# Conditioning sums, load distance and the start of a recurrence in a two-block network

## Chip, cores and metric

One core of one Trainium2 chip runs the whole kernel as one program. The metric is device time in microseconds (us): the median of the runs of a kernel. Trace times below are us from the start of the span of one profiled execution.

## What is computed

An input of 256 rows by 1024 columns passes through two blocks in 32-bit floats. The first block has a sparse attention and convolution mixer and a gated feed-forward layer. The second has two layers of three sublayers: feed-forward, mixer, feed-forward. The mixer of its first layer is a differential attention, that of its second a gated linear recurrence. Shortened:

```
for layer in range(2):
    mod = (silu(c) @ ada_w[layer] + ada_b[layer]).reshape(1, 3, 3, 1024)   # shift, scale, gate of each sublayer
    x = x + 0.5*gate0 * swiglu(rms(x)*(1+scale0) + shift0)      # feed-forward
    h = rms(x)*(1+scale1) + shift1
    x = x + gate1 * (diff_attention(h) if layer == 0 else hgrn2(h))
    x = x + 0.5*gate2 * swiglu(rms(x)*(1+scale2) + shift2)      # feed-forward
```

The recurrence `hgrn2` has 8 heads of 128. Per head it needs a query product and a forget product of h. The forget gates decay a running state along the 256 rows, and the values are summed with these decays. A gate product and an output product follow.

## The kernel before

**Products.** TensorE multiplies with each operand split in a high and a low part: `whi` is ScalarE's cast of the weights (L200), `wlo` is VectorE's difference (L213), and each product is three matmuls (high by high, high by low, low by high). Weights come in 1 MB pieces through `Stream`, in one fixed order: five feed-forward layers of 33 pieces each, the attention's 16 pieces (`w_qk`, `w_v`, `w_o`), the recurrence's 20. `load_to` issues a load on SP's queue into the pool `raw`, which has five buffers. `next` (L216) hands out piece i, issues loads up to piece i + `loads` (2 unless said) and splits ahead.

**Conditioning sums.** The 24 vectors `mod` (shift, scale, gate) are weights times `silu(c)`. They are computed piece by piece beside the rest: one part of a vector is a 1 MB load (`adaraw`, L522, in the same five buffers and on the same queue) and two VectorE instructions of 128x1024 that add into `adacc` (L549 for the first of a vector, L551 for the others). Four parts make a vector. Then `reduce` sums over the partitions with TensorE (L571 for a gate, L574 for a shift or scale) and VectorE adds the bias. `ADA_PLAN` (L501) is a list of (step, parts): at each weight piece `ada_step` (L503) compares the parts loaded with a straight line through that list, loads at most one more, and sums at most one that was loaded in an earlier step. The step is the number of the weight piece plus 8. The attention's pieces are 74 to 89, so its steps are 82 to 97; those of the third and fourth feed-forward sublayer are 98 to 130 and 131 to 163.

**Which vector is reduced where.** Each sublayer gets lists of vectors: `early` for the feed-forward loop, reduced when their parts are summed, `scale` for a mixer's output product, reduced between its pieces (`out_product`), and `fill` for a sublayer's end. Parts 52 to 55 belong to vector 15, 56 to 59 to vector 16, 60 to 63 to vector 17, 68 to 71 to vector 19, 80 to 83 to vector 22. Vectors 15 and 16 are the shift and scale for the recurrence layer's first sublayer, needed at the end of the third feed-forward sublayer; 19 is needed at the end of the fourth.

**Attention.** Four times a product for two heads (`rows_half`, `ps_qk`), the sums of squares, a power on GpSimd (`qss`, L631), the normalised rows (`qk`, L1660), transposes (`ps_qkT`), scores, softmax (`s`, `a`), transposes. Then the value products and the output product. Here the planner orders the instructions of each engine by its own estimate of when they are due.

**Recurrence.** Its order is written by hand (`order(True)`) up to the end of its main loop; what stands behind the loop (gate and value products) the planner may issue between. Work goes by pairs of heads, g = 0 to 3. `heads(g)` makes the forget product (`ps_f`, four pieces of 12 matmuls) and the query product (`ps_q`, four pieces) and computes the forget gates on ScalarE and VectorE in steps between the query's pieces. Pair 0 runs through `heads(0)` alone. Then a loop over g takes the diagonal product (`ps_d`, L1855) and eight levels: exponentials on ScalarE (`hX`, L1865), products and prefix sums on VectorE (L1867 to L1873), one piece of later pairs' work (`next(fill)`, L1875), and a product of the level (`ps_l`, L1882, at the last level L1885) that VectorE copies under a mask. `work` deals out pairs 1 to 3, 24 pieces in all, over the 32 levels.

Of the kernel before, what the change touches and what calls it, by code (L numbers as in the profile page):

```python
# [168 lines left out]
class Stream:  # L169
# [46 lines left out]
    def next(self, ahead=3, loads=2, ada=True):  # L216

        i = self.at
        self.at += 1
        self.split_to(2 * i + 1)  # L220
        self.load_to(i + loads)
        if ada:
            self.net.ada_step(i + 8)
        self.split_to(2 * i + 1 + ahead)
        self.load_to(i + loads)
        return [self.parts.pop(2 * i), self.parts.pop(2 * i + 1)]
# [188 lines left out]
class Net:  # L415
# [82 lines left out]
        mm(out, wl, xh, start=False, stop=last)  # L498


    ADA_PLAN = ((0, 0), (8, 0), (14, 12), (36, 24), (56, 36), (76, 48), (93, 60), (126, 72), (159, 84), (184, 84), (204, 88))  # L501

    def ada_step(self, i):  # L503
        for (a, na), (b, nb) in zip(self.ADA_PLAN, self.ADA_PLAN[1:]):
            if a <= i <= b:
                goal = na + (nb - na) * (i - a) / (b - a)
                break
        else:
            goal = 88
        before = self.ada_loaded  # L510
        if self.ada_loaded < min(goal, 88):
            self.ada_load()
        self.ada_to(min(before, self.ada_done + 1))
# [197 lines left out]
    def rows_half(self, name, done):  # L711

        acc = [self.psum("acc", f"{name}{t}") for t in range(2)]
        xh, xl = self.h
        for j in range(2):
            parts = self.W.next()
            for k in range(4):
                f = 4 * j + k
                for t in range(2):
                    self.rows_mm([acc[t]], parts[k // 2], t, (xh[:, f], xl[:, f]), f == 0, f == KT - 1, (k % 2) * 512)  # L720
        for t in range(2):
            done(t, acc[t])
# [1036 lines left out]
    def hgrn(self, end, scale, fill):  # L1759
        nc, T, tc, W = self.nc, self.T, self.tc, self.W  # L1760
        with ExitStack() as es:
# [7 lines left out]
            ac = m1.tile([P, 4, 2, P], F32, name="hac")  # L1769
            def product(name, done):  # L1770

                parts = W.next(ahead=1)
                ps = self.psum("acc", name)
                for n in range(2):
                    for piece in self.feat_pieces(ps, parts, n * S, n * P):
                        if n and piece == 0:
                            W.split_to(2 * W.at + 1)
                        if n and piece == 1:
                            done(ps)
                        yield  # L1780
# [44 lines left out]
            def work():  # L1825
                for g in range(1, 4):
                    yield from heads(g)
# [13 lines left out]
            if True:  # L1841
                for _ in heads(0):
                    pass
                nc.gpsimd.tensor_copy(levels, wide)
                fill = work()
                late = []
                for g in range(4):
                    (pre, suf, kk), q = gates.pop(g), qs.pop(g)
                    A = at[:, g].rearrange("p t e s -> p (t e) s")

                    pd = self.psum("t", "ps_d")
                    for t in range(2):
                        for e in range(2):
                            o = (2 * t + e) * P
                            nc.tensor.matmul(pd[:, o:o + P], kk[:, e, t * P:(t + 1) * P], q[:, e, t * P:(t + 1) * P], start=True, stop=True)  # L1855

                    def diagonal(A=A, pd=pd):
                        nc.vector.tensor_tensor(out=A, in0=pd.rearrange("p (a b) -> p a b", a=4),
                                                in1=self.ident[:, None, :].to_broadcast([P, 4, P]), op=ALU.mult)
                    late.append(diagonal)  # L1860
                    for a, m in enumerate(LEVELS + (P,)):
                        nb = 2 * S // (2 * m)
                        blk = lambda x: x.rearrange("p a b -> p (a b)").rearrange("p (n c) -> p n c", c=2 * m)
                        X = self.w512("hX").rearrange("p (a b) -> p a b", a=2)
                        nc.scalar.activation(blk(X)[:, :, m:], blk(pre)[:, :, m:], AF.Exp)  # L1865
                        nc.scalar.activation(blk(X)[:, :, :m], blk(suf)[:, :, :m], AF.Exp)
                        nc.vector.tensor_tensor(out=blk(X)[:, :, m:], in0=blk(q)[:, :, m:], in1=blk(X)[:, :, m:], op=ALU.mult)  # L1867
                        if m < P:

                            sb, pb = blk(suf), blk(pre)  # L1870
                            nc.vector.tensor_tensor(out=sb[:, :, :m], in0=sb[:, :, :m],
                                                    in1=pb[:, :, 2 * m - 1:2 * m].to_broadcast([P, nb, m]), op=ALU.add)
                            nc.vector.tensor_tensor(out=pb[:, :, m:], in0=pb[:, :, m:],  # L1873
                                                    in1=pb[:, :, m - 1:m].to_broadcast([P, nb, m]), op=ALU.add)
                        next(fill, None)  # L1875
                        pd = self.psum("bt"[a % 2], "ps_l")
                        if m < P:
                            for t in range(2):
                                for e in range(2):
                                    o = (2 * t + e) * P  # L1880
                                    x = X[:, e, t * P:(t + 1) * P]
                                    nc.tensor.matmul(pd[:, o:o + P], x, x, start=True, stop=True)  # L1882
                        else:
                            for e in range(2):
                                nc.tensor.matmul(pd[:, e * P:(e + 1) * P], X[:, e, :P], X[:, e, P:], start=True, stop=True)  # L1885
                        late.pop()()

                        def store(A=A, a=a, g=g, pd=pd):
                            if a < len(LEVELS):
                                nc.vector.copy_predicated(A, levels[:, a:a + 1, :].to_broadcast([P, 4, P]),  # L1890
                                                          pd.rearrange("p (a b) -> p a b", a=4))
                            else:
                                nc.scalar.copy(ac[:, g], pd[:, :2 * P].rearrange("p (a b) -> p a b", a=2))
                        late.append(store)
                    late.pop()()
                for _ in fill:
                    pass
# [26 lines left out]
    def run(self):  # L1924
        stop = self.stop
        self.nvec = {None: 24, "m1": 5, "b1": 9, "f00": 14, "da": 17, "f02": 20, "f10": 23, "hg": 24}[stop]
        self.start()
        self.first_mixer()
        if stop == "m1":
            return self.dump()  # L1930
        early = lambda *v: [x for x in v if x < self.nvec]
        with self.tc.tile_pool(name="lnr", bufs=1) as lp:
            rows = self.ln_rows(lp, 1)
            self.ffn(0, End(self, G2, 1.0, self.mods(0, 0), rows, "ln_rms"), [G2, 6, 7], early(8))
        if stop == "b1":
            return self.dump()
        with self.tc.tile_pool(name="bias", bufs=1) as bp:
            with self.tc.tile_pool(name="bias0", bufs=1) as small:
                self.ffn(1, End(self, 8, 0.5, self.mods(0, 1), mixer="ps_qk"), [9, 10] + early(13), early(12, 11),
                         self.attention_setup(bp, small))  # L1940
            if stop == "f00":
                return self.dump()
            self.diff_attention(bp, End(self, 11, 1.0, self.mods(0, 2)), *early(16), early(15, 14))
        if stop == "da":
            return self.dump()
        self.ffn(2, End(self, 14, 0.5, self.mods(1, 0)), early(19), early(18, 17))
        if stop == "f02":
            return self.dump()
        self.ffn(3, End(self, 17, 0.5, self.mods(1, 1), mixer="ps_i"), early(22), early(21, 20))
        if stop == "f10":  # L1950
            return self.dump()
        self.hgrn(End(self, 20, 1.0, self.mods(1, 2)), None, ())
        if stop == "hg":
            return self.dump()
        self.ffn(4, End(self, 23, 0.5, None), early(23))
# [21 lines left out]
```

## Time and profile before

| what | us |
|---|---|
| median of three runs | 1467.81 (1466.42 to 1471.65) |
| the profiled execution | 1466.25 |
| its span | 1464.4 |
| attention | 566 to 706 |
| third and fourth feed-forward sublayer | 706 to 1090 |
| recurrence | 1090 to 1270 |

The span is the time from the first to the last instruction of the profiled execution. The borders of the sublayers are rounded and taken from the first and last matmuls of their products. In the profile PE is TensorE, PEld its weight loads, DVE is VectorE, ACT is ScalarE, POOL is GpSimd and SP issues the loads; PEclk is the granted TensorE clock as a share of full speed. A windows row has a stretch, its length, the busy us and instructions of PE, PEld, DVE, ACT and POOL (an engine without work in it may be missing), then PEclk, the DMA share and GB/s.

### The profile page before, as it was taken

To read this page: it belongs to the slowest core of one execution; us is meant where nothing else is said; L and a number is where in the kernel's file an instruction comes from. 1 tells how busy PE (TensorE), PEld (TensorE's weight loads), DVE (VectorE), ACT (ScalarE), POOL (GpSimd) and SP (SyncE) were. 2 spreads that over 40 slices of the span, in tenths; PEclk is the share of its full clock that TensorE was granted. 3 is DMA by queue.
4 is the path that set the end of the run, shared out by engine and by line. 5 is a ranking of instruction groups with operands and counts; after the bars stand their busy time and mean duration, and the time that the engine had idled before them with its cause. 6 is when DMAs were issued, how large, how long until landed. Compare 5 with 4: busy or idle time off the path is not lost.

```text
span 1464.4 us, 22646 instructions
## 1 busy us (share of the span) xinstructions
PE 1405.5 (96%) x9154; PEld 1254.3 (86%) x9154; DVE 1095.0 (75%) x1691; ACT 709.3 (48%) x1217; POOL 46.6 (3%) x45
## 2 busy tenths in 40 slices
PE   7999899999899999889999999999998999999998
PEld 6875888997899897667999998999987988899997
DVE  5888678778797777889876667865676998765555
ACT  5544533444544446466544445544455676454442
POOL 0001000000000000122000000000000001000000
PEclk9999899999999999999999999999999999999999
DMA  8866578777398875756486664766644244266640
GB/s 310 344 228 255 202 277 315 274 284 256 126 347 329 312 291 216 258 202 230 144 314 247 258 249 184 281 255 259 254 186 144 87 144 170 90 219 255 229 174 30
DMA packets 51354, 337.87 MB, mean 231 GB/s; under 512 B 5761, under 2 KB 7553, under 8 KB 13105
## 3 DMA queue, kind: packets, MB, share of 16 engines
q1 hardware_dynamic: 51104, 336.35, 62.0%
q8 instruction: 72, 1.18, 0.3%
q14 instruction: 34, 0.27, 0.1%
q10 hardware_dynamic: 144, 0.07, 0.0%
HBM read 335.33 MB, written 1.06 MB: 230 GB/s over the span
## 4 chain that ended last, share of the span: by engine, by line
PE 74%; DVE 15%; ACT 4%; issue 3%; POOL 3%; DMA 1%; POOLq 0%; SPq 0%; DVEq 0%; ACTq 0%
PE ps_dn L693 19%; PE ps_up L655 13%; PE ps_up L657 13%; PE ps_up L654 12%; DVE wlo L213 3%; PE ps_up L865 2%; DVE adacc L551 2%; PE ps_att L693 2%; PE ps_wo L709 1%; POOL qss L631 1%; PE ps_up L872 1%; ACT whi L200 1%; PE ps_do L693 1%; PE ps_g L693 1%; POOL oss L631 1%
## 5 line engine op out<-in xcount | busy, mean ns | idle before, releaser
L213 DVE TENSOR_TENSOR wlo<-raw,whi 128x1024 fp32r<-128x1024 f32 (+2 forms) x414 | 485.0, 1208 | 51.8 <-ACT whi L200 51.3
L200 ACT CAST whi<-raw 128x1024 fp32r<-128x1024 f32 (+2 forms) x414 | 412.7, 1038 | 132.4 <-issue 45.5
L655 PE MATMUL ps_up<-xh,wlo 128*128 128x256 f32 x1600 | 392.7, 283 | 3.9 <-DVE wlo L213 3.8
L654 PE MATMUL ps_up<-xh,whi 128*128 128x256 f32 x1600 | 393.7, 284 | 0.4 <-ACT whi L200 0.4
L655 PEld LDWEIGHTS ps_up<-xh,wlo 128*128 128x128 f32 x1600 | 306.1, 191 | 7.5 <-DVE wlo L213 4.7
L654 PEld LDWEIGHTS ps_up<-xh,whi 128*128 128x128 f32 x1600 | 305.8, 191 | 3.9 <-ACT g L962 0.9
L657 PE MATMUL ps_up<-xl,whi 128*128 128x256 f32 x1600 | 224.4, 283 | 0.0
L657 PEld LDWEIGHTS ps_up<-xl,whi 128*128 128x128 f32 x1600 | 206.2, 192 | 0.0
L551 DVE SCALAR_TENSOR_TENSOR adacc<-adaraw,cact,adacc 128x1024 f32<-128x1024 f32 x154 | 197.4, 1282 | 4.4 <-DMA gate<-in_ada_b_dram 1.6
L962 ACT ACTIVATE g<-ps_up 128x256 f32<-128x256 f32 x100 | 38.5, 385 | 317.0 <-PE ps_up L657 317.0
L693 PE MATMUL ps_dn<-whi,hh 128*128 128x512 f32 x440 | 174.0, 395 | 0.0
L693 PE MATMUL ps_dn<-wlo,hh 128*128 128x512 f32 x440 | 172.9, 393 | 0.6 <-DVE wlo L213 0.6
L964 DVE TENSOR_TENSOR hu<-ps_up,g 128x256 f32<-128x256 f32 x100 | 42.3, 423 | 154.0 <-ACT g L962 153.8
L693 PE MATMUL ps_dn<-whi,hl 128*128 128x512 f32 x440 | 140.7, 394 | 0.0
L693 PEld LDWEIGHTS ps_dn<-whi,hl 128*128 128x128 f32 x440 | 82.6, 188 | 18.6
L693 PEld LDWEIGHTS ps_dn<-wlo,hh 128*128 128x128 f32 x440 | 82.8, 188 | 18.3 <-DVE wlo L213 1.0
L693 PEld LDWEIGHTS ps_dn<-whi,hh 128*128 128x128 f32 x440 | 83.1, 189 | 17.0 <-issue 0.2
L638 DVE TENSOR_TENSOR hl<-hu,hh 128x256 fp32r<-128x256 f32 x100 | 42.5, 425 | 47.2 <-ACT hh L637 47.2
L637 ACT CAST hh<-hu 128x256 fp32r<-128x256 f32 x100 | 40.7, 407 | 70.6 <-DVE hu L964 70.6
L631 POOL TENSOR_TENSOR rstd<-rstd,mhalf 128x1 f32<-128x1 f32 x16 | 9.7, 605 | 874.2 <-DVE rstd L303 641.0
L369 ACT ACTIVATE xh<-ps_tr,vcol,modA 128x128 fp32r<-128x128 f32 x48 | 18.1, 457 | 30.6 <-PE ps_tr L358 25.7
L1882 PE MATMUL ps_l<-hX 128*128 128x128 f32 x224 | 29.8, 276 | 0.6 <-DVE hX L1867 0.6
(340 smaller groups left out, 1857.6 us busy)
## 6 DMA issues: line engine op xcount, KB each, us to landing
raw<-in_up_dram SPq DMA_DIRECT2D x110, 1024.0 KB, 6.5
adaraw<-in_ada_dram SPq DMA_DIRECT2D x88, 1024.0 KB, 5.9
raw<-in_down_dram SPq DMA_DIRECT2D x55, 1024.0 KB, 6.3
adas<-in_ada_s_dram SPq DMA_DIRECT2D x8, 1024.0 KB, 6.5
raw<-in_w_qk_dram SPq DMA_DIRECT2D x8, 1024.0 KB, 6.2
raw<-in_w_att_dram SPq DMA_DIRECT2D x8, 724.0 KB, 7.8
wraw<-in_w_conv_dram SPq DMA_DIRECT2D x8, 512.0 KB, 10.8
gate<-in_ada_b_dram SPq DMA_DIRECT2D x8, 512.0 KB, 8.0
```

The source lines that it names most:

```text
L200: net.nc.scalar.copy(hi[:, :n], src)
L213: self.net.nc.vector.tensor_tensor(out=lo[:, :n], in0=src, in1=hi.bitcast(F32)[:, :n], op=ALU.subtract)
L551: nc.vector.scalar_tensor_tensor(out=acc, in0=raw[:, k], scalar=c[:, 2 * j + k:2 * j + k + 1], in1=acc, op0=ALU.mult, op1=ALU.add)
L631: self.nc.gpsimd.tensor_tensor(out=out, in0=in_, in1=self.mhalf[:, :n], op=ALU.pow)
L637: nc.scalar.copy(hi, src)
L638: nc.vector.tensor_tensor(out=lo, in0=src, in1=hi.bitcast(F32), op=ALU.subtract)
L654: mm(o, hi[:, at(k)], xh[:, k], start=k == 0, stop=False)
L655: mm(o, lo[:, at(k)], xh[:, k], start=False, stop=False)
L657: mm(o, parts[k // 4][0][:, at(k)], xl[:, k], start=False, stop=k == KT - 1)
L693: mm = lambda *args, **more: self.nc.tensor.matmul(*args, **more, **kw)
L962: self.last_silu = nc.scalar.activation(g, ps[:, :S], AF.Silu)
L964: nc.vector.tensor_tensor(out=u, in0=ps[:, S:], in1=g, op=ALU.mult)
```

## The change

Three edits.

1. Vector 16 is no longer reduced in the attention's output product but in the loop of the third feed-forward sublayer. Vector 19 moves from that loop into the one of the fourth, which now reduces 19 and 22. The plan of the parts is changed to match: up to step 82 it runs on nearly as before (52 parts), then 56 parts at step 98 in place of 60 at step 93, 70 at 131 in place of 72 at 126, 84 at 160 in place of 159.
2. `rows_half` (attention, and the gate and value products of the recurrence) and the query and forget products of the recurrence issue loads up to four pieces ahead, not two.
3. In the recurrence, four of the 24 pieces (the forget product of pair 1) are issued after pair 0's `heads` and before the loop over g.

```diff
-    ADA_PLAN = ((0, 0), (8, 0), (14, 12), (36, 24), (56, 36), (76, 48), (93, 60), (126, 72), (159, 84), (184, 84), (204, 88))
+    ADA_PLAN = ((0, 0), (8, 0), (14, 12), (36, 24), (56, 36), (82, 52), (98, 56), (131, 70), (160, 84), (184, 84), (204, 88))
...
         for j in range(2):
-            parts = self.W.next()
+            parts = self.W.next(loads=4)
...
             def product(name, done):
 
-                parts = W.next(ahead=1)
+                parts = W.next(ahead=1, loads=4)
...
                 fill = work()
+
+                for _ in range(4):
+                    next(fill)
                 late = []
...
-            self.diff_attention(bp, End(self, 11, 1.0, self.mods(0, 2)), *early(16), early(15, 14))
+            self.diff_attention(bp, End(self, 11, 1.0, self.mods(0, 2)), None, early(15, 14))
...
-        self.ffn(2, End(self, 14, 0.5, self.mods(1, 0)), early(19), early(18, 17))
+        self.ffn(2, End(self, 14, 0.5, self.mods(1, 0)), early(16), early(18, 17))
...
-        self.ffn(3, End(self, 17, 0.5, self.mods(1, 1), mixer="ps_i"), early(22), early(21, 20))
+        self.ffn(3, End(self, 17, 0.5, self.mods(1, 1), mixer="ps_i"), early(19, 22), early(21, 20))
```

## Rows read from the trace of the kernel before

**Rows 1.** The page, busy time, share and instructions of each engine.

```profile
PE 1405.5 (96%) x9154; PEld 1254.3 (86%) x9154; DVE 1095.0 (75%) x1691; ACT 709.3 (48%) x1217; POOL 46.6 (3%) x45
```

**Rows 2.** Windows by stage: stretch, length, busy us of each engine.

```profile
566.00:706.00 140.00, 126.67 (x623) 96.33 (x622) 122.56 (x273) 78.42 (x173) 27.98 (x15) 0.99 0.60 216
706.00:1090.00 384.00, 383.76 (x2701) 358.25 (x2699) 272.53 (x337) 182.17 (x274) 1.64 (x3) 1.00 0.65 242
1090.00:1270.00 180.00, 167.95 (x1082) 148.17 (x1081) 145.92 (x260) 108.13 (x208) 7.46 (x8) 0.99 0.37 131
```

**Rows 3.** Waits in the attention: us in total, times, longest.

```profile
DVE qk L1660 <- POOL qss L631: 11.0, 8, 1.8
...
PE ps_qkT L1665 <- DVE qk L1660: 4.5, 4, 1.4
```

**Rows 4.** The chain that ended last, attention: start us, us, what.

```profile
605.59 1.20 DVE adacc L551
...
635.29 0.66 DVE adacc L549
...
645.92 1.19 DVE adacc L551
...
693.69 0.44 PE ps_red L574 x4
```

**Rows 5.** Windows of tile adacc alone: attention's halves, feed-forward.

```profile
566.00:635.00 69.00, 3.13 (x12) 1.67 (x12) 14.81 (x12) 0.00 (x0) 0.98 0.60 222
635.00:706.00 71.00, 1.20 (x8) 1.00 (x8) 11.71 (x10) 0.00 (x0) 1.00 0.60 210
...
706.00:1090.00 384.00, 7.57 (x40) 5.04 (x40) 56.31 (x46) 0.00 (x0) 1.00 0.65 242
```

**Rows 6.** Busy us in two pieces of the attention, columns as in rows 2.

```profile
610.00:635.00 25.00, 23.25 (x116) 17.71 (x115) 21.21 (x49) 15.37 (x34) 7.43 (x3) 1.00 0.77 286
...
660.00:680.00 20.00, 19.56 (x117) 16.42 (x116) 18.77 (x45) 13.97 (x26) 3.97 (x2) 1.00 0.64 236
```

**Rows 7.** Timeline of GpSimd, attention: start, us, instruction, idle before it.

```profile
583.79 1.65 POOL L631 TENSOR_TENSOR qss<-qss,mhalf 128x8 f32<-128x8 f32 x1 [6.59 <-DVE qss L1657]
...
613.06 2.48 POOL L631 TENSOR_TENSOR qss<-qss,mhalf 128x8 f32<-128x8 f32 x1 [21.14 <-DVE qss L1657]
...
647.40 2.54 POOL L631 TENSOR_TENSOR qss<-qss,mhalf 128x8 f32<-128x8 f32 x1 [8.75 <-DVE qss L1657]
```

**Rows 8.** Transfers issued in the attention: count, size, median us to landing.

```profile
adaraw<-in_ada_dram SPq DMA_DIRECT2D x9, 1024.0 KB, 4.9
```

**Rows 9.** SP queue's waits, attention (two rows), then recurrence.

```profile
SPq L186 <- DVE wlo L213: 59.3, 13, 12.7
SPq L522 <- DVE wlo L213: 19.1, 3, 11.0
...
SPq L186 <- DVE wlo L213: 155.7, 19, 13.5
```

**Rows 10.** Waits in the recurrence: us in total, times, longest.

```profile
PE ps_l L1885 <- DVE hX L1867: 3.2, 2, 1.6
...
ACT whi L200 <- DMA raw<-in_w_ho_dram: 1.6, 1, 1.6
```

**Rows 11.** Timeline of TensorE at the start of the recurrence.

```profile
1122.55 0.28 PE L667 MATMUL ps_q<-xh,whi 128*128 128x256 f32 x1
...
1130.86 1.13 PE L1855 MATMUL ps_d<-hkq 128*128 128x128 f32 x8 [2.40 <-issue]
```

**Rows 12.** Timeline of ScalarE, the same place.

```profile
1110.56 3.88 ACT L200 CAST whi<-raw 128x1024 fp32r<-128x1024 f32 x4
```

**Rows 13.** Timeline of VectorE, the same place.

```profile
1114.05 5.76 DVE L213 TENSOR_TENSOR wlo<-raw,whi 128x1024 fp32r<-128x1024 f32 x5
```

**Rows 14.** Busy us late in the recurrence, columns as in rows 2.

```profile
1192.00:1218.00 26.00, 26.00 (x165) 22.92 (x164) 25.36 (x45) 18.07 (x35) 0.00 (x0) 1.00 0.48 163
1218.00:1242.00 24.00, 23.31 (x123) 19.63 (x122) 18.37 (x29) 14.27 (x19) 3.15 (x3) 1.00 0.51 172
```

## Prediction

> **What bounds the kernel now.** I read the busy shares first, then the stages, then each touched stage's waits, chain and queues. Over the whole span TensorE is busy 1405.5 of 1464.4 us and VectorE 1095.0 [rows 1], so the average says that only TensorE matters. The stages say more [rows 2]. In the attention (566 to 706 us) TensorE is busy 126.67 of 140 us and VectorE 122.56: TensorE loses 13.3 us there, and something else decides. In the two feed-forward sublayers behind it (706 to 1090 us) TensorE is busy 383.76 of 384 us and VectorE 272.53: this is TensorE's stretch, with 111 us of VectorE free. The recurrence sublayer (1090 to 1270 us) is between the two: TensorE 167.95 of 180, VectorE 145.92.
>
> Who keeps TensorE waiting in the attention? The longest entry is a result of VectorE, 4.5 us for "qk" [rows 3]. The chain in the same stretch [rows 4] runs through VectorE and, at 1.2 us an instruction, through its conditioning sums ("adacc"). So in this stage VectorE's order of work decides, and sums stand in it.
>
> **The sums that leave the attention.** 22 instructions of the sums run in the attention, 12 before 635 us (14.81 us) and 10 after it (11.71 us) [rows 5]. Under the old plan the counter of parts goes from 52 to 61 over the steps of this stage, under the new one from 52 to 56. The ten instructions after 635 us are vector 16 (one of 0.66 us and seven of 1.2 us) and the first two of vector 17; these go. The last three parts of vector 15, six instructions that stood in the first half, now come one part in four steps and fall into the second. VectorE loses 11.7 us of sums, and about 1.3 us for the two reductions and the bias of vector 16.
>
> What is that worth? I count only sums that stand on the chain, and no more than TensorE stood idle in that piece. After 635 us the chain holds four: 0.66 us at 635.29 and 1.19 us three times, the first at 645.92 [rows 4]. The other two fall into 660 to 680, where TensorE is busy 19.56 of 20 us [rows 6], so they are worth 0.44 together, not 2.38. That leaves 0.66 + 1.19 + 0.44 = 2.3 us; six postponed instructions take up about half of the ten places again, so 1.15. The transposes of vector 16 (two pieces on the chain, 0.44 us each [rows 4]) leave the output product: 0.9 us. Before 635 us five sums of vector 15 stand on the chain, the first at 605.59 [rows 4], 6 us together, but TensorE is idle only 1.75 us in 610 to 635 [rows 6]: 1.75. The sums earlier than that belong to parts that both plans have loaded by then, so they stay. Together 3.8 us. Bounds: nothing, if the next wait is just behind; 13.3 us, all that TensorE stood idle.
>
> One thing may add to it. A power on GpSimd takes 1.65 us at 583.79, where VectorE runs nothing beside it, and 2.54 us at 647.40, where a sum had just started [rows 7]. Three powers of the stage start behind a sum; without one each could be 0.9 us shorter, 2.7 us at most. But behind a split of the weights they are as long (2.48 us at 613.06 [rows 7]), and splits will often take the place; I add 0.7 us. By the Trainium skill, page "SBUF — State Buffer", section "Who interferes with whom", a VectorE instruction with two SBUF inputs shares a read port with a GpSimd instruction that reads SBUF, and whichever started first blocks the other; the 2.54 against 1.65 us agrees with it, and by it alone the sum would get 2.7 us here instead of 0.7 if no split followed.
>
> Attention: 4.5 us less.
>
> **Where the sums go.** Vector 16 and the start of 17 go into the third feed-forward sublayer, and the end of 19 with its reduction slides into the fourth. That is 10 instructions (11.7 us of VectorE) over 384 us in which 111 us are free [rows 2]; 46 such instructions run there already (56.31 us) [rows 5] beside a TensorE that is full. If that cover were gone they would cost their 11.7 us. Five 1 MB loads go with them, on SP's queue between the sublayers' weight loads; 384 us at 242 GB/s are 93 MB [rows 2], so they add one part in eighteen. One more transposed reduction stands in a feed-forward sublayer and one less in the attention: 0.9 us gained above is charged again here. Net the sums are worth 3.6 us.
>
> **Loads four ahead.** The SP queue only issues; a load waits there until its buffer is free. In the attention SP waited 59.3 us for weight splits to free one of the five buffers, in the recurrence 155.7 us [rows 9]. So the queue already stands as deep as its buffers allow, and an issue written two products earlier moves nothing unless the order among weight loads and sums' loads changes. What a deeper queue could win is bounded by the casts' longest wait for weights in the recurrence, 1.6 us [rows 10]. What it could cost is the rival on the ring of buffers below. I take nothing.
>
> **A quarter of the next heads first.** The recurrence works on pairs of heads; eight pieces of the next pair's products are dealt out between the eight levels of the present one. Now four pieces (the forget product of pair 1) run before pair 0's levels. TensorE starts pair 0's query product at 1122.55, and the next instruction behind it, the diagonal product, starts at 1130.86 after 2.40 us idle [rows 11]: the 48 matmuls took 5.9 us. The four pieces are 48 such matmuls. They fill the 2.40 us and push the diagonal product 3.5 us back. ScalarE gets the two casts of the next weights (four took 3.88 us [rows 12], so 1.94) ahead of the first exponentials, and VectorE their two splits (five took 5.76 us [rows 13], so 1.15 each) ahead of the first level's product. That product moves by at most 1.94 + 1.15 = 3.1 us, with 2.3 us less to do behind it: 0.8 us lost for VectorE.
>
> From then on every pair has its work four levels early. Levels four to seven of pair 2 have no fill left, and pair 3 has none, as before. In pair 3 the gate and value products already fill TensorE, issued between the levels by the planner: 26.00 of 26 us busy in 1192 to 1218, VectorE 25.36 [rows 14]. I expect the same products in the empty half of pair 2. Then TensorE does the same work with 2.40 us less idle and VectorE is 0.8 us later: 1.6 us less. Bounds: 5.6 us less if the 3.2 us of waits at the last levels [rows 10] vanish too, since the forget gates are ready earlier; 3.5 us more if nothing fills the freed half. I lean to the gain, because after 1218 TensorE (23.31 of 24 us) and not VectorE (18.37) is the nearer bound [rows 14].
>
> **Sum.** 3.6 + 0 + 1.6 = 5.2 us less. The profiled execution took 1466.25 us: its span of 1464.4 and 1.85 around it. That makes 1461.05; the median of the runs is 1.56 above the profiled one, so I forecast 1462.6 us, 0.36% less. Half a per cent (7.3 us) is about what a measurement of this kernel can tell from no change; below 1460.5 is faster, above 1475.1 slower.
>
> **Rivals.**
> *VectorE really is the attention's bound.* Its work comes off one for one: 11.7 + 1.3 = 13 us less, which TensorE's 13.3 idle just allows, with 0.9 back in the feed-forward stretch, and 1.6 in the recurrence: 13.7 us, 1454.1. For it: VectorE is busy 88% there. Against: 660 to 680 has almost no idle TensorE, and 11.0 us of VectorE's own idle time are waits for powers [rows 3], which a sum that leaves hardly shortens.
> *Nothing in the attention.* The next wait stands just behind: the power's round trip and the softmax keep TensorE as late as now. Then the time is between 1.6 less and 3.5 more, say 1467. For it: "qk", TensorE's longest wait, comes directly behind a power [rows 3]. The Trainium skill, page "Perfetto Trace Analysis", section "Identifying the Most-Contended Engine", would have one work on the engine with the highest occupancy first, which over the span is TensorE, and the change takes nothing from it: by that rule alone the time stays 1467.8. Its next section allows that this engine differs from stretch to stretch, and the stage rows [rows 2] agree with that.
> *Slower: the ring of five buffers.* Weights and sums share five buffers. With four weights ahead a sum's load stands behind more of them, gets a buffer only when a weight is split, and lands 4.9 us after its issue [rows 8]; VectorE works in order, so a late sum holds the softmax behind it. Four parts are left in the stage: all four late by a transfer make 19.6 us more, 1482.2. It decides the sign from the second late one (9.8 against 5.2) and passes half a per cent from the third (14.7, 1477.3). For it: a sum's load already waits for a split, up to 11.0 us [rows 9]. Against: fewer sums go through the ring, and VectorE's waits in the stage, powers first [rows 3], name no transfer.
>
> **Chances.** Forecast 0.46 (nearly half of it below 1460.5; its own range is 1457 to 1467); VectorE bound 0.17; nothing in the attention 0.27; ring 0.10, of which 0.06 beyond half a per cent. So faster 0.38, same 0.56, slower 0.06. For 8 in 10 I take 1454 to 1472: all but the far end of the first rival and most of the ring.
>
> **What would show it.** Right: ten or so sum instructions fewer between the first attention product and the output product; TensorE's idle time there down from 13.3 to about 9; the feed-forward stretch still full; the diagonal product of pair 0 about 3.5 us later with no idle before it, and the last levels of pair 3 about 2 us earlier; SP's issue times in the recurrence as before. Wrong: VectorE waiting for "adaraw" transfers in the attention; TensorE idle in the second half of pair 2; waits for powers growing by what the sums gave up; "ps_red" in the feed-forward sublayers waiting for its sums.

## The result and the profile after

The changed kernel takes 1479.61 us (median of 4 runs, 1478.36 to 1481.70) against 1467.54 for the kernel before in the same session: ratio 1.0079, 95% interval 1.0063 to 1.0094. It is 12 us slower; 1462.6 was forecast, in a range up to 1472. The profiled execution has a span of 1477.1 us, 12.7 more than before.

The page of the changed kernel, busy time of each engine, answers [rows 1]:

```profile
PE 1412.1 (96%) x9154; PEld 1259.1 (85%) x9154; DVE 1097.1 (74%) x1691; ACT 708.4 (48%) x1217; POOL 40.3 (3%) x45
```

Its windows by stage answer [rows 2], columns as there. The stages have moved, so the stretches are 570 to 716, 716 to 1109 and 1109 to 1284:

```profile
570.00:716.00 146.00, 128.54 (x615) 96.51 (x614) 110.73 (x258) 78.77 (x174) 21.72 (x15) 0.98 0.46 165
716.00:1109.00 393.00, 389.94 (x2735) 363.20 (x2733) 291.98 (x361) 184.16 (x279) 2.17 (x4) 1.00 0.70 256
1109.00:1284.00 175.00, 164.99 (x1068) 145.62 (x1067) 142.29 (x251) 106.99 (x207) 6.92 (x7) 0.99 0.36 127
```

VectorE has lost 12 us of work in the attention (122.56 to 110.73), and TensorE stands idle longer beside it: 146 - 128.54 = 17.5 us, where it was 13.3. The feed-forward stretch, full before, is now short by 393 - 389.94 = 3.1 us.

The windows of the sums alone in the changed kernel (two halves of the attention, then the feed-forward sublayers) answer [rows 5]:

```profile
570.00:640.00 70.00, 3.13 (x12) 1.67 (x12) 9.69 (x8) 0.00 (x0) 0.95 0.53 194
640.00:716.00 76.00, 0.00 (x0) 0.00 (x0) 2.56 (x2) 0.00 (x0) 1.00 0.40 139
716.00:1109.00 393.00, 8.83 (x48) 5.86 (x48) 70.60 (x58) 0.00 (x0) 1.00 0.70 256
```

Ten instructions are left in the attention instead of 22, so twelve went and not ten. The waits of the changed kernel in the attention (us in total, times, longest) answer [rows 3]:

```profile
DVE qk L1660 <- POOL qss L631: 13.1, 8, 1.8
...
PE ps_qkT L1665 <- DVE qk L1660: 8.4, 6, 1.6
```

The transposes of the query-key blocks now wait six times and 8.4 us instead of four and 4.5. VectorE waits 13.1 / 8 = 1.6 us for each power, which is as long as a power takes (1.64 or 1.65 us for five of the eight): it has little else to do meanwhile.

Stage by stage I compare lengths, not times of day, since the clock's changes before 380 us shift everything behind them by some microseconds between executions. The stages run from the second "diag" instruction of VectorE (end of the first feed-forward sublayer) to the first product of the attention (mostly the second feed-forward sublayer), to the start of the last matmul of the output product, to the first product of the recurrence sublayer, and to the start of its last output matmul:

| kernel | second feed-forward | attention | third and fourth | recurrence | ratio and interval |
|---|---|---|---|---|---|
| before | 194.3 | 134.9 | 389.9 | 170.6 | |
| after | 199.2 | 140.6 | 393.8 | 169.3 | 1.0079 (1.0063 to 1.0094) |
| loads | 194.5 | 135.4 | 389.9 | 171.2 | 1.0006 (0.9993 to 1.0019) |
| sums | 199.1 | 137.9 | 395.4 | 169.0 | 1.0082 (1.0063 to 1.0101) |
| quarter | 194.2 | 134.9 | 389.9 | 169.3 | 0.9996 (0.9982 to 1.0010) |
| after-old-to-76 | 195.1 | 130.8 | 395.2 | 169.3 | 0.9997 (0.9987 to 1.0007) |
| v15-by-92 | 195.9 | 132.0 | 390.7 | 167.9 | 0.9975 (0.9961 to 0.9990) |
| v15-by-92-no-loads | 194.3 | 131.0 | 390.7 | 169.3 | 0.9976 (0.9962 to 0.9989) |
| v15-as-before | 194.2 | 135.3 | 390.7 | 167.8 | 0.9994 (0.9984 to 1.0003) |
| v15-as-before-no-loads | 195.8 | 135.0 | 390.7 | 169.1 | 0.9997 (0.9981 to 1.0014) |
| one-sum-later | 196.0 | 130.8 | 391.1 | 171.7 | 0.9989 (0.9975 to 1.0003) |
| one-sum-later-quarter | 196.0 | 130.7 | 391.2 | 169.0 | 0.9970 (0.9957 to 0.9982) |
| v15-half-slope | 194.0 | 133.9 | 390.8 | 169.1 | 0.9985 (0.9972 to 0.9998) |
| v15-half-slope-less | 195.4 | 132.2 | 390.7 | 169.3 | 0.9979 (0.9964 to 0.9994) |
| before-no-powers | 195.9 | 127.5 | 389.8 | 170.3 | 0.9940 (0.9923 to 0.9956) |
| after-no-powers | 199.4 | 128.3 | 395.4 | 169.2 | 0.9997 (0.9987 to 1.0007) |

By these two traces the change costs 4.9 + 5.7 + 3.9 and gives 1.3 back. About 1.6 of the 4.9 need not come from the change. In ten of the sixteen traces, that of the changed kernel among them, TensorE's clock is lower just behind the second "diag", inside this stage (mean granted clock 0.79 over 374 to 382 us in the changed kernel, 1.00 in the kernel before). before-no-powers, up to the attention the same program as the kernel before, has it too and takes 195.9 us. Of the ten, the three with the new plan take 199.1 to 199.4 us and the other seven 195.1 to 196.0.

**The second feed-forward sublayer** was charged nothing, and it changed first. The timeline of the changed kernel's SP queue there (start, us to issue):

```profile
448.16 0.56 SPq L186 DMA_DIRECT2D raw<-in_up_dram  x1
448.77 0.42 SPq L522 DMA_DIRECT2D adaraw<-in_ada_dram  x1
449.24 0.42 SPq L525 DMA_DIRECT2D gate<-in_ada_b_dram  x1
449.76 0.62 SPq L186 DMA_DIRECT2D raw<-in_up_dram  x1
```

VectorE, ScalarE and TensorE behind it (start, us, instruction, idle before it):

```profile
457.08 2.60 DVE L551 SCALAR_TENSOR_TENSOR adacc<-adaraw,cact,adacc 128x1024 f32<-128x1024 f32 x2
459.60 1.22 DVE L213 TENSOR_TENSOR wlo<-raw,whi 128x1024 fp32r<-128x1024 f32 x1
...
460.28 1.99 ACT L200 CAST whi<-raw 128x1024 fp32r<-128x1024 f32 x2 [2.62 <-DMA raw<-in_up_dram]
...
460.87 0.39 PE L655 MATMUL ps_up<-xh,wlo 128*128 128x256 f32 x1 [2.06 <-DVE wlo L213]
```

The SP queue at the same place in the kernel before:

```profile
447.15 0.90 SPq L186 DMA_DIRECT2D raw<-in_up_dram  x2
448.14 0.38 SPq L522 DMA_DIRECT2D adaraw<-in_ada_dram  x1
448.58 0.60 SPq L525 DMA_DIRECT2D gate<-in_ada_b_dram  x1
```

The new segment of the plan runs from (56, 36) to (82, 52), 0.615 parts a step instead of 0.6, and here that brings a part one step forward. Its load and the gate's then stand between two weight loads instead of behind both. TensorE then stands 2.06 us for a split of its weights, the one at 459.60. The cast for this split had ended at 457.66 us, but on VectorE two sums stand ahead of it. In the kernel before, two splits come first (456.56 us) and the two sums follow them (458.83 us). The second weight is late as well, and a cast waits 2.62 us for it, but its splits follow the wait of TensorE (from 461.37 us on); what this lateness would cost by itself no run shows. The two windows, the changed kernel first and the one before second, show that TensorE comes back at a lower clock (mean granted clock 0.93 instead of 1.00, between its levels of 1.2 and 2.4 GHz):

```profile
455.00:480.00 25.00, 22.94 (x147) 21.31 (x146) 19.42 (x21) 11.47 (x15) 0.00 (x0) 0.93 1.01 388
```
```profile
455.00:480.00 25.00, 24.96 (x180) 23.53 (x179) 20.53 (x22) 12.10 (x16) 0.00 (x0) 1.00 0.99 387
```

**The third feed-forward sublayer** starts with a wait. VectorE's and TensorE's timelines in the changed kernel:

```profile
723.32 2.60 DVE L551 SCALAR_TENSOR_TENSOR adacc<-adaraw,cact,adacc 128x1024 f32<-128x1024 f32 x2
...
725.97 1.09 PE L574 MATMUL ps_red<-ident,adacc 128*128 128x128 f32 x8 [2.82 <-DVE adacc L551]
```

The last part of vector 15 is loaded at step 95, at 671.9 us, as the last part in the attention; its two sums run only at 723.32 us, directly ahead of the transposes that need them.

### The profile page after: what moved, and what is told of

Its sections match the earlier page's. It is cut to its first block, busy times and chain, and to the rows that moved or that the text cites. A ratio compares the mean times of both kernels' runs of the same rounds, so it can differ in the third digit from the quotient of the medians.

```text
span 1477.1 us, 22648 instructions
## 1 busy us (share of the span) xinstructions
PE 1412.1 (96%) x9154; PEld 1259.1 (85%) x9154; DVE 1097.1 (74%) x1691; ACT 708.4 (48%) x1217; POOL 40.3 (3%) x45
## 4 chain that ended last, share of the span: by engine, by line
PE 77%; DVE 14%; ACT 3%; issue 3%; POOL 2%; DMA 1%; SPq 0%; POOLq 0%; DVEq 0%; ACTq 0%
PE ps_dn L693 18%; PE ps_up L657 12%; PE ps_up L655 12%; PE ps_up L654 12%; DVE wlo L213 4%; PE ps_up L865 2%; PE ps_att L693 2%; DVE adacc L551 1%; PE ps_wo L709 1%; PE ps_up L872 1%; PE ps_g L693 1%; POOL qss L631 1%; PE ps_do L693 1%; PE ps_qk L693 1%; PE ps_l L1885 1%
## 5 line engine op out<-in xcount | busy, mean ns | idle before, releaser
L693 PEld LDWEIGHTS ps_dn<-wlo,hh 128*128 128x128 f32 x440 | 82.8, 188 | 17.3 <-issue 0.2
```

The costliest lines, as they stand in the source:

```text
L693: mm = lambda *args, **more: self.nc.tensor.matmul(*args, **more, **kw)
```

## Experiments

**One part of the change at a time.** Three kernels, each the kernel before with one part of the diff.

```
loads:    self.W.next()  ->  self.W.next(loads=4);   W.next(ahead=1)  ->  W.next(ahead=1, loads=4)
sums:     ADA_PLAN and the lists of vectors as in the change
quarter:  fill = work();  for _ in range(4): next(fill)
```

> Only the loads four ahead in both mixers, the rest as before. My theory (the new plan of the sums costs the time, the loads nothing): the first attention product starts at 570.4 us as before, the attention (first product to the last one of the output product, 132 us before) changes by under 1.5 us, the recurrence by under 0.5, the median stays within 1.5 us of the kernel before (ratio 0.999 to 1.001). Rival (the deeper loads are what disturbs the attention, since weights then stand ahead of the sums' loads in the five buffers): the attention takes 5 to 6 us longer and the ratio is 1.003 to 1.004.

> Only the conditioning sums moved (new plan and new lists), loads and recurrence as before. My theory: the first attention product starts 4.4 us later (a sum's load stands ahead of a weight load in the second feed-forward sublayer), the attention takes 4 to 6 us longer although 10 sum instructions have left it, the third feed-forward sublayer starts 3 to 4 us later still (the reduction of vector 15 waits for its sums), nothing after that: 12 to 14 us more, ratio 1.008 to 1.010. Rival (the loads make the attention slower): about 8 us more, ratio 1.0055, with an attention as long as before. Rival of the prediction (the sums are worth 3.6 us): ratio 0.9975.

> Only the quarter of the next heads first, the rest as before. My theory: everything up to the first product of the recurrence at its old time, then 1.3 to 1.6 us less up to the last product of that sublayer: ratio 0.999. Rival (the quarter first is worth the 4.3 us that the changed kernel regains behind pair 0's first product, and the loads take 3 of them back): 4 us less, ratio 0.997. Rival (the gain there comes from the loads): 0, ratio 1.000.

The loads alone are worth nothing; the sums alone give the whole loss (ratio 1.0082, each of the three stages hit); the quarter first takes 1.3 us from its stage, which its ratio of 0.9996 cannot tell from nothing. In the attention the sums alone cost 3.0 us, less than the 4 to 6 expected, and 5.7 together with the loads, in another order and at a lower clock (0.98 instead of 0.99); in the next stage the kernel with the sums alone is the one at the lower clock. So deeper loads are not what makes the attention longer, but with the sums moved they change how much longer. The 1.6 us that the recurrence is shorter with the sums alone goes with the clock of that stretch (mean 1.00 there, 0.99 before) and is no gain of the change. At like clock the quarter's gain is seen in the traces: at 1.00 the recurrence takes 167.8 and 167.9 us with it and 169.0 without, at 0.99 it takes 169.0 to 169.3 with it and 170.3 and 170.6 without.

**The old plan up to step 76.**

```
(56, 36), (82, 52), (98, 56)   ->   (56, 36), (76, 48), (82, 52), (98, 56)
```

> The changed kernel with the old line of the plan up to step 76, and the parts of 52 at step 82 as in the new one, so that the loads of the second feed-forward sublayer go out in the old order. My theory: the first attention product is back at 570.4 to 571.4 us (3.4 to 4.4 us earlier than in the changed kernel), no wait of the up product for its weights at 460 us; the third feed-forward sublayer still loses 2.8 us to the wait of a reduction; the attention has another order of work and may differ by 3 us either way: 1472 to 1479 us, ratio to the kernel before 1.003 to 1.008. Rival (the 4.4 us there are a state of the clock or the loads as such): the first product stays at 574.8 us, ratio 1.008.

The loads in the second feed-forward sublayer go out in the old order, its wait is gone, and the stage takes 195.1 us instead of 199.2. What I had not expected by its size: the attention takes 130.8 us, 9.8 less than in the changed kernel, with as many sums in it (ten, as there), and the time is 1467.56 us where 1472 to 1479 was expected. So one point in the plan takes back all 12 us. The wait of the reduction remains (2.83 us).

**The end of vector 15**, its last part loaded at step 90 instead of 95 by the plan's line, or at 86 as in the kernel before, each with and without the deeper loads.

```
v15-by-92:       ... (76, 48), (84, 52.6), (92, 56), (98, 56) ...
v15-as-before:   ... (76, 48), (87.3, 56), (98, 56) ...
-no-loads:       the same without loads=4
```

> The changed kernel with the plan at its old line up to step 76 and the parts of vector 15 all loaded by step 92 instead of 95 (the next vector from step 98 as in the changed kernel), so that its two last sums stand in the attention and not at the start of the third feed-forward sublayer. My theory: the wait of the reduction there (2.8 us of TensorE) goes, and from the last instruction of the output product to the first product of the recurrence it takes 390 us as in the kernel before instead of 393.8 to 395.4; the attention has two more sums (2.6 us of VectorE) and yet another order, 131 to 135 us; the recurrence takes 169.3. Sum 1460 to 1465 us, ratio to the kernel before 0.995 to 0.998. Rival (the third feed-forward sublayer loses the time to the added loads and the order, not to that wait): it still takes 394 us, ratio 1.000.

> The changed kernel with the plan at the old line until vector 15 is loaded (step 87), the next vector from step 98 on. All sums up to vector 15 stand then where they stood, and only vector 16 and the start of 17 leave the attention. My theory: attention 131 to 134 us (134.9 in the kernel before), feed-forward 390, recurrence 169.3: 1461 to 1466 us, ratio 0.995 to 0.999. Rival (which order the planner finds decides the attention, whatever the sums do): anything from 130 to 141 us there, so a ratio up to 1.003.

> As the kernel with vector 15 by step 92, but with the loads two ahead as in the kernel before. My theory (loads four ahead are worth nothing but another order in the attention): the recurrence takes 169 us with or without them, the feed-forward sublayers 390; the attention differs from the one with the loads by up to 4 us either way, and the ratio lies between 0.994 and 0.999. Rival (the deeper loads are needed once the sums are gone): the attention takes over 4 us longer and shows waits for the casts of the weights.

> The kernel before with the quarter first and with vector 16 and the start of 17 moved out of the attention, nothing else: the plan is the old line until vector 15 is loaded, the loads are two ahead. The order on TensorE up to the value product is then that of the kernel before. This is the prediction's step alone (10 sums off the second half of the attention, its estimate 3.3 us for them with the reduction). My theory: 132 us in the attention instead of 134.9, 390 in the feed-forward sublayers, 169.3 in the recurrence: ratio 0.996 to 0.998. Rival (a sum that leaves moves the wait to the powers): attention 134.5 to 135, ratio 0.999. Rival (order): attention longer than before.

All four take 390.7 us in the third and fourth feed-forward sublayers: the wait for vector 15 is what cost there, and the 0.8 us that is left over fits the added reduction (TensorE is busy 390.38 us in v15-as-before, 389.55 before). The two with "as before" are the prediction's step as nearly as a plan can make it: vector 16 and the start of 17 have left, and the other sums stay in their stage. Their attention takes 135.3 and 135.0 us, not less than 134.9 and not the 131 to 134 and 132 expected. The windows of v15-as-before, attention, all instructions, then the sums alone:

```profile
570.20:705.50 135.30, 121.64 (x587) 92.11 (x588) 107.29 (x252) 75.21 (x167) 23.99 (x14) 0.99 0.52 183
```
```profile
570.20:705.50 135.30, 3.13 (x12) 1.67 (x12) 14.82 (x12) 0.00 (x0) 0.99 0.52 183
```

VectorE works 107.29 us in it, where the kernel before has 118.07 between the same two instructions, and TensorE's idle time is 13.7 us against 13.1. Those ten sums were worth nothing in the order that the planner made without them. That order is the old one only as far as the third block (without the deeper loads); in the last block the second transposes follow the first after 2 products instead of 9. What the sums would be worth in the old order throughout, no run shows.

**No sum leaves; early ones come later.**

```
before:   (76, 48), (93, 60)   ->   (76, 48), (82, 52), (93, 60)
```

By the two lines three loads (parts 50, 52 and 55) go out one step later.

> The kernel before with one point put into its plan (52 parts at step 82, then 60 at step 93 as before): every sum stays in the sublayer in which it was, but one load goes out one product later at the attention's start, and one sum less stands ahead of the first block's softmax on VectorE. My theory (one sum ahead of the first block's probabilities makes TensorE wait 1.8 us there and drop to its lower clock for 10 us): the first half of the attention (first product to last query-key product) takes 66 to 68 us instead of 70.5, the attention 131 to 133 instead of 134.9, the ratio is 0.997 to 0.999. Rival (what the sums are worth they are worth by leaving, wherever they stood): attention 134 to 136, ratio 1.000.

The attention takes 130.8 us with all 22 sums in it. Windows of a piece in the first blocks of the attention, 30 us behind its first product, in the kernel before and in this one:

```profile
600.40:612.40 12.00, 9.72 (x37) 7.71 (x38) 12.00 (x24) 6.46 (x14) 0.00 (x0) 0.86 0.85 315
```
```profile
602.40:614.40 12.00, 11.39 (x53) 9.12 (x52) 11.32 (x19) 7.44 (x16) 1.67 (x1) 1.00 0.92 337
...
572.40:703.20 130.80, 119.08 (x596) 90.68 (x596) 115.95 (x261) 74.79 (x167) 26.82 (x13) 1.00 0.61 221
```

In the kernel before VectorE is busy for all of the 12 us, TensorE stands 2.3 and the mean granted clock is 0.86; here TensorE stands 0.6 and holds its clock. Over the attention (last row) 2.7 of the 4.1 us are busy time of TensorE (119.08 against 121.79) and 1.4 idle time; the clock of the 12 us accounts for 0.14 x 12 = 1.7 of them, so the lower level lasted well under the 10 us expected. The gain is not all kept: in the next stage TensorE waits 1.1 us for the normalised rows behind the attention, and the stage takes 391.1 us instead of 389.9. In the median 1.2 us are left (1466.27 against 1467.48), which this run cannot tell from nothing. TensorE's timeline of the kernel before names the wait:

```profile
601.81 0.50 PE L1705 MATMUL ps_aT<-ident,a 128*128 128x128 f32 x2 [1.78 <-DVE a L1702]
```

The sums of one part fewer (four instructions, 5.11 us, instead of six, 7.14, in the first 32 us) stand ahead of the first block's probabilities. The planner's order differs too: 26 products instead of 15 stand on TensorE between the transposes of the second half of the first block and those of the probabilities. This run doesn't part the two; the next ones help.

Two further plans were meant to thin out the first blocks more.

```
v15-half-slope:        ... (76, 48), (84, 52), (92, 56), (98, 56) ...    quarter first, loads two ahead
v15-half-slope-less:   ... (76, 47), (84, 51), (93, 56), (98, 56) ...
```

> The kernel before with the quarter first and the sums moved, the loads two ahead, the plan at one part in two steps from step 76 on until vector 15 is loaded at step 92: against the kernel with vector 15 by step 92, another sum less stands in the attention's first blocks. My theory: as good as that one within 2 us (attention 129 to 133, feed-forward 390.7, recurrence 169), ratio 0.996 to 0.998. Rival (each sum that leaves the first blocks is worth its 1.2 us): attention 128 to 129, ratio 0.995.

> As the last one, with one part fewer loaded by step 76 (47 at step 76, 51 at 84, 56 at 93). My theory: within 2 us of the last one, ratio 0.995 to 0.998. Rival (the last part comes too late again): TensorE waits 2.8 us for the reduction at the start of the third feed-forward sublayer, ratio 0.999 or above.

Attention 133.9 and 132.2 us. The plans did not do what they were meant to: parts put off in the stage ahead reach the attention, and its first 60 us hold 10 and 11 sum instructions, against 9 in v15-by-92-no-loads. Whether fewer early sums would be worth more stays untested. But the two runs part sums and order for the wait at the first block's probabilities. In the first 32 us they have 6.41 and 6.39 us of sums, and the probabilities come 31.4 and 30.9 us behind the stage's first product, no earlier than in the kernel before (30.9). Yet TensorE doesn't wait for them and the clock there stays at 1.00, since 27 products stand ahead of their transposes instead of 15. So the products that the planner puts there cover the wait. TensorE waits 2.0 and 1.5 us for a split of its weights instead.

**The powers left out.** Why is the attention of the changed kernel 5.7 us longer than before, with twelve sums fewer?

```
-  self.power(ss, ss)        # in the query-key norms
```

> The kernel before, with the eight powers of the query-key norms left out (the row factors go into the product unpowered, so the attention's scores are other numbers); the order of the product blocks on TensorE is the same as before. My theory: the waits of the query-key transposes for VectorE (4.5 us, 4 times) fall to 1 us or less and the attention gets 3 to 4 us shorter, 131 to 132 us. Rival (the softmax behind it takes the wait over): the attention stays above 134 us.

> The changed kernel with the same eight powers left out. My theory (the attention of the changed kernel loses its 5.8 us by meeting the transposes too soon after the sums of squares): their waits (8.4 us, 6 times) fall to 2 us or less, the second stretch of lower clock goes, and the attention takes 132 to 134 us, 7 to 9 us less than 140.6, within 2 us of the kernel before without powers. Rival (the loss lies in the order of the softmax and the weight splits on VectorE): it keeps 4 us or more over the kernel before without powers. The 4.4 us ahead of the attention and the 3.8 us behind it stay in any case.

Windows of the attention, first the kernel before without powers, then the changed one without them:

```profile
572.00:699.50 127.50, 121.91 (x596) 94.16 (x597) 118.17 (x265) 75.35 (x167) 8.70 (x6) 0.97 0.66 235
```
```profile
576.20:704.50 128.30, 121.75 (x588) 92.91 (x589) 105.84 (x250) 75.14 (x167) 6.90 (x6) 0.97 0.52 185
```

The gap of 5.7 us between the two kernels shrinks to 0.8. The transposes' waits for "qk" vanish in the first and are 0.2 us in the second. So 4.9 us of the loss are there only with the powers: they hold 7.4 us in the kernel before and 12.3 in the changed one. The pair is not quite clean, since without the powers the planner orders the changed kernel anew (in its last three blocks the second transposes follow the first after 5, 7 and 5 products instead of 6 each); the order of the kernel before changes only in a few instructions of the first block. With the powers the gap is idle time (17.3 against 13.1 us) and, for 1.5 us, busy time of TensorE, whose mean granted clock is 0.98 against 0.99. I had expected 131 to 132 us for the kernel before without powers and 132 to 134 for the changed one; both are shorter, though their clock is lower (0.97). The 7.4 us are more than the 4.5 of TensorE's waits that carry the powers' name.

**The quarter first with one sum later.** No sum leaves its sublayer.

> The kernel before with the one point in its plan that lets one load go out later at the attention's start, and the quarter of the next heads first; no sum leaves the sublayer that it stood in. My theory (leaving is worth nothing, the place of one sum in the first blocks is worth 4 us): attention 131, recurrence 169.3 to 170, ratio 0.997 to 0.999, as good as the kernels with vector 15 by step 92 (0.9975 and 0.9976) within their intervals. Rival (moving the sums is worth 2 us more): 0.9990 and above.

Ratio 0.9970 (1462.82 us): as fast as the best kernels with the sums moved (0.9975, 0.9976), 0.3% faster than the kernel before, clear of noise, and faster than the changed one. Moving the sums out of the attention isn't needed for any of it.

## Why the prediction was wrong

**The attention, 4.5 us less: the step that failed.** "I count only sums that stand on the chain, and no more than TensorE stood idle in that piece" takes for granted that the rest of the order stays and closes up. It did not: the planner ordered the stage anew, and the attention became 5.7 us longer with twelve sums fewer. With ten sums in it as well, but in another order, it takes 9.8 us less (after-old-to-76). Nor did the late sums pay where the first half of the stage kept its order (70.5 us in both): v15-as-before-no-loads has them gone and is no shorter, where the step gives 3.2 us (2.3 of sums and 0.9 of the reduction). Its last stretch, where the reduction was, did get 1.1 us shorter (27.4 against 28.5), but the value products ahead of it got 1.2 us longer. TensorE waits 5.5 us in these two stretches together, against 5.0 before, for the output norms, the softmax and the normalised keys instead of for "qk". The rival "nothing in the attention" was right there that the next wait stands just behind. The whole change went further than that rival. In each of the last three blocks the query-key transposes of the second row half follow those of the first after 6 products in the changed kernel, and after 10, 8 and 9 in the kernel before; TensorE reaches them before the power is back. By the no-power pair such waits are most of the loss; that the 6 products alone make them is argued, not shown, and after-old-to-76 speaks against so simple a rule: it has 10, 9 and 1 there, 4.6 us of these waits and 130.8 us. Why the planner puts them there the trace doesn't show. Waits for powers that grow were among the signs of being wrong.

**"By then both plans have loaded them, so they stay."** So they did: six instructions and 7.13 us of them run in the first 32 us of the changed kernel, six and 7.14 before. But the runs put the attention's possible gain just there. With three of the early loads one step later the stage takes 4 us less (one-sum-later), 1.7 of it through the clock, and the two half-slope runs show that the order that results, not the sum taken away, ends the wait there.

**The shorter powers, 0.7 us.** They did get shorter: GpSimd's busy time in the attention is 21.72 us instead of 27.98 [rows 2]. That is what the port rule of the Trainium skill ("SBUF — State Buffer", "Who interferes with whom") would give for sums that leave, and the trace agrees. But VectorE's waits for them rose from 11.0 to 13.1 us, so the time did not follow.

**The feed-forward sublayers, 0.9 us more.** 58 sum instructions run there beside TensorE, and behind the seam they cost nothing, as argued (TensorE is busy 390.38 of 390.70 us in v15-as-before, with 56 of them). The step that failed is the one on vector 15: its last part doesn't fall into the attention's second half but out of the stage. It was among the wrong signs ("ps_red" waiting for its sums), but priced nowhere: 2.82 us of wait, 3.1 in the stage beyond the 0.8 of the added reduction.

**The second feed-forward sublayer** has no term in the sum: I read the two plans by their values at the stages' ends and not by the steps between, where a difference of 0.015 parts a step brings a load one step forward and two sums ahead of a split. It cost 3 to 4 us, 2.06 of them the wait and 0.07 x 25 = 1.75 the clock behind it.

**Loads four ahead, nothing:** right by themselves (1.0006), and in the total with the sums moved (1.0079 with them, 1.0082 without). **The ring of buffers:** no wait of VectorE for a sum's transfer in the attention; what came late by a transfer was a weight, elsewhere. That this rival's 1477.3 to 1482.2 us hold the measured time is chance.

**The quarter first, 1.6 us less:** right in mechanism, 1.3 in size. The diagonal product in the changed kernel answers [rows 11]:

```profile
1148.12 1.05 PE L1858 MATMUL ps_d<-hkq 128*128 128x128 f32 x8
```

The 2.40 us ahead of it are gone. It stands 1148.12 - 1109.2 = 38.9 us behind the stage's first product, 3.2 later than before (3.5 forecast), and the end comes 1.3 earlier. Gate and value products fill the second half of pair 2, as forecast: TensorE stands idle 9.8 us in the stage instead of 11.8 (169.3 - 159.5 and 170.6 - 158.8).

**Left open:** what makes the planner choose among these orders, and what besides the clock and the wait of 1.78 us makes up the 4 us of one-sum-later.

## What to carry to other kernels

Where a planner orders a stage, taking work off a busy engine is not a subtraction: price it by the order that results, or expect several microseconds either way from one moved load. Compare an issue plan step by step with the queue that it feeds, since a part that comes one step sooner can put its load ahead of a weight's and sums ahead of a split, and one that comes a step too late is waited for at the next seam. Before sums are moved between stages, try moving one of them within its stage.

## What the hardware showed that was not expected

A short wait of TensorE can cost twice its length here. Around the 1.78 us at 601.81 and the 2.06 us at 460.87 the mean granted clock was 0.86 over 12 us and 0.93 over 25 us, which is 1.7 us lost each time, and stages without such a wait were 3 to 4 us shorter. Other waits leave the clock alone: around 2.82 us at 725.97 the mean over 716 to 750 us was still 1.00. The same wait in sums and after-old-to-76 (2.82 and 2.83 us) went with a mean of 0.95 over 36 us, and the third and fourth sublayer took 395.4 and 395.2 us there instead of 393.8. What decides between the two the runs don't show.
